# A Conformer layer on one core: the LayerNorm between the last convolution and the second projection, worked in token halves over all channels, with more of the last convolution's taps on the matrix engine

## The chip, the cores and the metric

The kernel runs on one core of a Trainium2 chip. A core has five engines that run side by side, each with its own queue of instructions in a fixed order: TensorE (matrix products, PE in the profile, its weight loads PEld), VectorE (DVE), ScalarE (ACT), GpSimd (POOL) and SyncE (SP), which here only issues transfers. TensorE writes its results into PSUM, eight banks of 512 float32 columns; all else lies in SBUF. The metric is the time of one execution on the device, in microseconds; less is better.

## The reference

One layer for 512 tokens of 2048 channels, all in float32: an RMS norm, a convolution module, a residual, then a squared-ReLU network of inner width 8192, a residual and a last RMS norm. The part that matters here:

```python
def conformer_conv(h, w_pw1, b_pw1, w_dw, b_dw, ln_g, ln_b, w_pw2, b_pw2):
    u = h @ w_pw1 + b_pw1
    a, gate = jnp.split(u, 2, axis=-1)
    u = a * jax.nn.sigmoid(gate)
    u = lax.conv_general_dilated(
        u, w_dw[:, None, :], window_strides=(1,),
        padding=[(CONV_WIDTH // 2, CONV_WIDTH // 2)],
        dimension_numbers=("NWC", "WIO", "NWC"),
        feature_group_count=D_MODEL) + b_dw
    u = jax.nn.silu(layer_norm(u, ln_g, ln_b))
    return u @ w_pw2 + b_pw2
```

The convolution has 31 taps for each channel. The layer norm takes its mean and variance over the 2048 channels of a token, so nothing of it can start for a token before the last channels have gone through the convolution.

## The kernel before, in words

Channels lie on the 128 partitions in 16 tiles (k or j = 0 to 15), tokens along the free dimension. A float32 product is made of three reduced-precision ones: each operand is split into a high part (a cast on ScalarE, `split_hi` for weights) and a low part (a subtraction on VectorE or GpSimd, `split_lo`); `mm3` issues high times high, high times low, low times high. The weights come in pieces of 512 KB (`wr`); a piece of the second projection holds two k tiles for 512 output channels.

**First projection and convolution.** For each channel tile j, `pw1` projects into two PSUM banks (pa and pg), `glu` makes the gated signal u, and `conv` sums 31 taps: some as a ScalarE product and a GpSimd add (`on_pool`), the rest as VectorE multiply-adds in two PSUM banks (`on_vector`), joined at the end. From the third tile on, the VectorE chain starts from `kb`, a bank of its own tag that holds a shift near the mean. `sums` adds value and square to running sums S and Q on GpSimd.

**The last tile (j = 15) is worked in token halves**, half 0 being tokens 0 to 255 and half 1 the rest. `pw1` runs for 272 tokens and then for the other 240 (as 256 columns). Of half 0's taps 7 are on GpSimd, 7 on TensorE (`conv_pe`: matmuls with a diagonal weight, `dgw`; in float32 each is two instructions) and 17 on VectorE; of half 1's 9, 8 and 14. In TensorE's order the taps of half 0 stand behind the whole projection, those of half 1 in three lots among the statistics.

**The layer norm.** Per half: `ln_sums` and `ln_last` sum S, Q, the last two values and squares over the partitions (matmuls of one column, 16 and 8 instructions, into the bank `cols`, which takes over the bank of `kb`); `ln_m2`, `ln_var`, `ln_guard` and `ln_power` make the inverse deviation on ScalarE, VectorE and GpSimd; `ln_mean` and `ln_scale` spread mean and deviation over the partitions by matmuls with diagonal matrices, and ScalarE copies the mean to SBUF. A unit (k, half) is then `ln_a` (GpSimd adds the negative mean), `ln_b` (VectorE multiplies by the deviation, ScalarE does Silu and the cast) and `ln_c` (VectorE subtracts for the low part). Before the change k = 0 to 7 are worked in halves and k = 8 to 15 at full width by `ln(k)`.

**The second projection** has four groups of 512 output channels with four banks each. In the first group the first four pieces (k = 0 to 7) run in halves: half 0 of all four, then half 1 of all four, then the other four pieces at full width. Hooks at given places (`LN_AT`) put the statistics of half 1 among half 0's matmuls: sums at the third piece, mean at the start of the fourth, deviation one block later. Everything behind is dense on TensorE.

**What sets the order.** TensorE's order is the order of the program text throughout. Inside a `manual_schedule(engines=ordered)` block the orders of VectorE, ScalarE and GpSimd are also those of the text; between such blocks, and for everything outside them, a planner merges by its own estimate of times. An engine never passes over a waiting instruction. Tiles of one tag share a ring of buffers: a new one waits until the old user of its buffer is done; the banks `mm` (4), `x` (3) and `y` (1) are such rings.

Of the kernel before, what the change touches and what calls it, by code (L numbers as in the profile page):

```python
# [34 lines left out]
LAST_POOL, LAST_PE = (7, 9), (7, 8)  # L35
# [5 lines left out]
PE_AT = (2, 4)  # L41
SPLIT_AT = (1, 4)
NEXT_AT = 7
TAIL = (20, 7, 4, 2, 3)
LN_AT = ((0, 2, 2), (0, 3, 0), (0, 3, 1))
# [6 lines left out]
def conformer_layer(ctx: ExitStack, tc: tile.TileContext, xT, vecs, wdw, w1, w2, wupb, wdn, outT):  # L52
# [337 lines left out]
    def conv_parts(j, npool, t0=0, n=T, npe=0):  # L390
# [61 lines left out]
    def conv_pe(acce, t0, n, i0, i1, npe):  # L452

        u = ubuf[(NK - 1) % 3]
        for i in range(i0, i1):
# [5 lines left out]
                start=i == 0,  # L461
# [4 lines left out]
    def shift():  # L466
# [3 lines left out]
        nc.tensor.matmul(box["kb"], lhsT=nmean, rhs=vg[0][:, 0, :], start=True, stop=True)  # L470

# [62 lines left out]
    banks_b = pw1(last, HT, HT)  # L534
# [8 lines left out]
    def ln_sums(h):  # L543
        t0 = HT * h
        colsum(cols, 4 * h, [S, box[last - 1][0]], t0, 2, h == 0, False, 1)
        colsum(cols, 4 * h + 2, [Q, box[last - 1][1]], t0, 2, False, False)

    def ln_last(h):
        t0 = HT * h
        colsum(cols, 4 * h, [vlast], t0, 2, False, True, 1)  # L550
        colsum(cols, 4 * h + 2, [sqlast], t0, 2, False, True)
# [4 lines left out]
    def ln_diag_mean(h):  # L556
        st[h]["dm"] = diag(cols[:, 4 * h : 4 * h + 2], f"mu{h}", ph1)

    def ln_mean(h):

        b = rstd[:, 0:HT]
        spread(st[h]["dm"], b, h == 1)
        nc.scalar.copy(out=mus[:, halves[h]], in_=b)

    def ln_m2(h):
        st[h]["m2"] = ph1.tile([P, 2], F32, name=f"m2{h}", bufs=1)
        nc.scalar.activation(out=st[h]["m2"], in_=cols[:, 4 * h : 4 * h + 2], func=AF.Square)

    def ln_var(h):
        st[h]["var"] = ph1.tile([P, 2], F32, name=f"var{h}", bufs=1)  # L570
        nc.vector.tensor_sub(out=st[h]["var"], in0=cols[:, 4 * h + 2 : 4 * h + 4], in1=st[h]["m2"])
# [23 lines left out]
    def ln_b(k, h):  # L595
        t = ph1.tile([P, T], F32, tag=("vt", "ta")[k % 2], name=f"lu{k}_{h}", bufs=2 - k % 2)[:, 0:HT]
# [11 lines left out]
    def ln(k):  # L608
        t = ph1.tile([P, T], F32, tag="pc", name=f"lt{k}")
        nc.gpsimd.tensor_add(out=t, in0=vg[k // 4][:, k % 4], in1=mus)  # L610
        t2 = ph1.tile([P, T], F32, tag="vt", name=f"lu{k}")
        for h in range(2):
            nc.vector.tensor_mul(out=t2[:, halves[h]], in0=t[:, halves[h]], in1=scale_of[h])
        s = ph1.tile([P, T], F32, tag="pm", name=f"ls{k}", bufs=3)
        nc.scalar.activation(out=s, in_=t2, func=AF.Silu, scale=col(C_LNG, k), bias=col(C_LNB, k))
        nc.scalar.copy(out=sh[k], in_=s)
        nc.vector.tensor_sub(out=sl[k], in0=s, in1=sh[k].bitcast(F32))

    with tc.manual_schedule(engines=ordered):

        acc0, rstd = bank("mm", "acce0"), bank("x", "acce1")
        npool, npe = LAST_POOL[0], LAST_PE[0]
        on_pool, on_vector, join, vt, pc = conv_parts(last, npool, 0, HT, npe)
        npool1, npe1 = LAST_POOL[1], LAST_PE[1]
# [8 lines left out]
        for c in range(npool):  # L633
            on_pool(c)
            if c in SPLIT_AT:
                split_hi(n_p1 + 1 + SPLIT_AT.index(c))
        for c in range(npool, TAIL[0]):
            on_vector(c)
        conv_pe(acc0, 0, HT, 0, npe, npe)
        glu(last, *(b[:, EDGE - HT : HT] for b in banks_b), EDGE)  # L640
        some(1)
        cols = bank("y", "cols")
        scale_of = cols[:, HT:T], rstd[:, HT:T]
        ln_sums(0)
        conv_pe(rstd, HT, HT, 0, PE_AT[0], npe1)
        for c in range(TAIL[0], CW - npe - 2):
            on_vector(c)
        v = vlast[:, halves[0]]
        nc.vector.tensor_add(out=v, in0=pc[-1], in1=acc0[:, halves[0]])
        for c in range(CW - npe - 2, CW - npe):  # L650
            on_vector(c)
        join()
        nc.vector.tensor_add(out=v, in0=v, in1=vt)

        for c in range(5):
            on_pool1(c)
            if c == 2:
                split_hi(n_p1 + 3)
        ln_square(0)
        for c in range(5, TAIL[1]):  # L660
            on_pool1(c)
        some(TAIL[2])
        ln_last(0)
        conv_pe(rstd, HT, HT, PE_AT[0], PE_AT[1], npe1)
        ln_m2(0)
        ln_diag_mean(0)
        ln_var(0)
        ln_guard(0)
        ln_power(0)
        some(3)  # L670
        ln_mean(0)

        nc.scalar.activation(out=tiny, in_=ones[:, 0:1], func=AF.Silu)
        ln_diag_scale(0)
        ln_scale(0)
        conv_pe(rstd, HT, HT, PE_AT[1], npe1, npe1)
        ln_a(0, 0)
        ln_a(1, 0)
        for c in range(TAIL[1], npool1):
            on_pool1(c)  # L680
        some(TAIL[3])
        for k in range(0, 8, 2):
            if k < 6:
# [375 lines left out]
```

## Time and profile before

| | |
|---|---|
| median of 3 runs (lowest to highest) | 1942.48 us (1941.43 to 1949.83) |
| the profiled execution's own time, its span | 1946.38 us, 1944.6 us |
| granted TensorE clock, mean | 0.992 |
| TensorE busy | 1913.9 us, 98% |
| VectorE, ScalarE, GpSimd busy | 1389.9 (71%), 741.1 (38%), 356.7 us (18%) |
| HBM read, written | 193.27 MB, 4.19 MB |

The span runs from the first to the last instruction; 1.8 us lie around it. The busy share is a mean over the whole run and says little of the short stretch between the first and the second projection, which comes at about 350 to 436 us. The granted clock has two levels, 1.00 (2.4 GHz) and half of it; a mean between them says for what share of a stretch the clock was low.

### The profile page before, as it was taken

Reading aid. Unit: us, or ns where it says so; the run is one execution under the profiler, and the core shown is the slowest. Engines: PE = TensorE matmul, PEld = TensorE weight load, DVE = VectorE, ACT = ScalarE, POOL = GpSimd, SP = SyncE. Lnnn points to the kernel's source line nnn. Section 1 sums busy time; section 2 is a strip of 40 time slices with the busy share of each in tenths; the row PEclk is TensorE's granted clock in tenths of the full one; section 3 lists DMA queues with packets and bytes.
Section 4 is the critical chain, followed back from the end, with each engine's and each line's share of the span. In section 5 each row is a group of like instructions: output and inputs, shape, how many; then the busy total and the mean of one; then the engine's idle time right before and its main releaser. Section 6 shows DMA issues by size and latency. Waiting matters only on the chain.

```text
span 1944.6 us, 27603 instructions
## 1 busy us (share of the span) xinstructions
PE 1913.9 (98%) x11192; PEld 1702.6 (88%) x11192; DVE 1389.9 (71%) x1911; ACT 741.1 (38%) x907; POOL 356.7 (18%) x243
## 2 busy tenths in 40 slices
PE   9999999899999999999999999999999999999997
PEld 7888888888879898998989899898989989899987
DVE  6999999875467675766767576676757667576844
ACT  6544444554344232423324233332423324242443
POOL 1789998741120000000000000000000000000000
PEclk9999999999999999999999999999999999999999
DMA  7332333143322333333233232323323233332332
GB/s 245 98 98 87 98 98 110 43 141 96 98 78 79 117 101 91 113 87 110 86 108 109 88 119 79 118 87 103 115 87 109 87 119 93 92 116 89 109 98 99
DMA packets 134558, 199.23 MB, mean 102 GB/s; under 512 B 7200, under 2 KB 72992, under 8 KB 134432
## 3 DMA queue, kind: packets, MB, share of 16 engines
q1 hardware_dynamic: 134288, 197.41, 33.1%
q8 instruction: 87, 1.43, 0.3%
q14 instruction: 39, 0.32, 0.1%
q10 hardware_dynamic: 144, 0.07, 0.0%
HBM read 193.27 MB, written 4.19 MB: 102 GB/s over the span
## 4 chain that ended last, share of the span: by engine, by line
issue 70%; PE 25%; DVE 4%; ACT 1%; POOL 1%; DMA 0%; SPq 0%; POOLq 0%; DVEq 0%; ACTq 0%
PE g L201 3%; PE g L202 3%; PE g L200 3%; PE pa L202 2%; PE pa L201 2%; PE pa L200 2%; PE pg L202 2%; PE pg L201 2%; PE pg L200 2%; DVE acc L426 2%; PE pa L363 1%; PE pg L363 1%; DVE slot L604 0%; POOL Q L841 0%; DMA wr<-w 0%
## 5 line engine op out<-in xcount | busy, mean ns | idle before, releaser
L162 ACT CAST wh<-wr 128x1024 fp32r<-128x1024 f32 x215 | 226.0, 1051 | 451.0 <-PE g L201 315.3
L200 PE MATMUL g<-z,wh 128*128 128x512 f32 (+1 forms) x1016 | 390.6, 384 | 0.0
L201 PE MATMUL g<-z,wh 128*128 128x512 f32 (+1 forms) x1016 | 390.3, 384 | 0.0
L202 PE MATMUL g<-z,wl 128*128 128x512 f32 (+1 forms) x1016 | 390.1, 384 | 0.0
L167 DVE TENSOR_TENSOR wl<-wr,wh 128x1024 fp32r<-128x1024 f32 x157 | 197.1, 1256 | 214.4 <-ACT wh L162 214.2
L202 PE MATMUL u<-slot,wl 128*128 128x256 f32 x1120 | 320.1, 286 | 3.6 <-DVE wl L186 2.6
L200 PE MATMUL u<-slot,wh 128*128 128x256 f32 x1120 | 318.1, 284 | 0.0
L201 PE MATMUL u<-slot,wh 128*128 128x256 f32 x1120 | 317.9, 284 | 0.0
L186 DVE TENSOR_TENSOR wl<-ws,wh 128x1024 fp32r<-128x1024 f32 x128 | 156.9, 1225 | 188.0 <-ACT wh L185 187.0
L248 POOL TENSOR_TENSOR rr_fin<-ms_fin,mhalf 128x2 f32<-128x2 f32 x2 | 1.4, 697 | 1341.5 <-DVE ms_fin L246 1341.5
L185 ACT CAST wh<-ws 128x1024 fp32r<-128x1024 f32 x128 | 134.4, 1050 | 289.9 <-DVE ws L183 135.1
L426 DVE SCALAR_TENSOR_TENSOR acc<-u,wd,acc 128x512 f32<-128x512 f32 (+1 forms) x362 | 239.0, 730 | 3.2 <-ACT acc L422 2.5
L202 PEld LDWEIGHTS g<-z,wl 128*128 128x128 f32 x1016 | 190.9, 188 | 37.8
L200 PEld LDWEIGHTS g<-z,wh 128*128 128x128 f32 x1016 | 191.0, 188 | 37.5
L201 PEld LDWEIGHTS g<-z,wh 128*128 128x128 f32 x1016 | 191.0, 188 | 37.1
L202 PEld LDWEIGHTS u<-slot,wl 128*128 128x128 f32 x1120 | 216.1, 193 | 7.4 <-DVE wl L186 6.6
L200 PEld LDWEIGHTS u<-slot,wh 128*128 128x128 f32 x1120 | 216.2, 193 | 0.0
L201 PEld LDWEIGHTS u<-slot,wh 128*128 128x128 f32 x1120 | 216.1, 193 | 0.0
L202 PE MATMUL u<-T,wl 128*128 128x256 f32 x672 | 190.6, 284 | 1.6 <-DVE wl L186 1.5
L200 PE MATMUL u<-T,wh 128*128 128x256 f32 x672 | 190.7, 284 | 1.0 <-ACT wh L185 1.0
L201 PE MATMUL u<-T,wh 128*128 128x256 f32 x672 | 190.1, 283 | 0.0
L178 ACT CAST wh<-wr 128x768 fp32r<-128x768 f32 x128 | 106.9, 835 | 214.5 <-PE g L201 123.0
(199 smaller groups left out, 3448.8 us busy)
## 6 DMA issues: line engine op xcount, KB each, us to landing
wr<-wupb SPq DMA_DIRECT2D x128, 512.0 KB, 3.6
wr<-wdn SPq DMA_DIRECT2D x128, 512.0 KB, 3.7
wr<-w SPq DMA_DIRECT2D x128, 256.0 KB, 3.2
wr<-w SPq DMA_DIRECT2D x32, 512.0 KB, 3.6
h<-xT SPq DMA_DIRECT2D x4, 1024.0 KB, 11.3
outT<-h SPq DMA_DIRECT2D x14, 256.0 KB, 2.8
x<-xT SPq DMA_DIRECT2D x6, 512.0 KB, 8.1
x<-xT SPq DMA_DIRECT2D x4, 256.0 KB, 4.9
```

The source lines that it names most:

```text
L162: nc.scalar.copy(out=prepped[i][0], in_=r)
L167: eng.tensor_tensor(out=lo, in0=r, in1=hi.bitcast(F32), op=ALU.subtract)
L178: nc.scalar.copy(out=hr, in_=r[:, :, 1:4])
L185: nc.scalar.copy(out=hs, in_=s)
L186: nc.vector.tensor_tensor(out=ls, in0=s, in1=hs.bitcast(F32), op=ALU.subtract)
L200: nc.tensor.matmul(out, lhsT=wh, rhs=xh, start=start, stop=False, **kw)
L201: nc.tensor.matmul(out, lhsT=wh, rhs=xl, start=False, stop=False, **kw)
L202: nc.tensor.matmul(out, lhsT=wl, rhs=xh, start=False, stop=stop, **kw)
L248: nc.gpsimd.tensor_tensor(out=r, in0=ms, in1=mhalf[:, 0:n], op=ALU.pow)
L363: nc.tensor.matmul(banks[j][s], lhsT=w[:, s, k % 2, c], rhs=x, start=k == 0 and x is ah[k] and w is wh, stop=stop)
L426: nc.vector.scalar_tensor_tensor(out=acc if c < end - 1 else vt, in0=u[:, c : c + n], scalar=wd[:, j, c : c + 1], in1=src, op0=ALU.mult, o ...
```

## The change

- For the last tile TensorE takes 10 taps of half 0 and 14 of half 1; VectorE is left with 14 and 8. The taps of half 0 are now emitted from within the second projection half of the last tile, ahead of its k = 8 (`first_taps`, hooked at `LAST_AT`), and the bank for them is taken from the ring ahead of the two banks of that half.
- The second half of the shift is copied to SBUF (`kbs`), so that `kb`'s bank has no reader left when the column sums of half 0 want it. Each half has its own bank for its four columns of sums (`stat`): `cols` for half 0, the bank of half 1's TensorE taps for half 1. The sums of half 1 are made together, at the hook.
- All 16 channel tiles go through the layer norm in halves, as one list of 32 units (`units`): first k = 0 to 15 of half 0, then of half 1. `ln_step` issues the adds up to three units ahead, the multiply, Silu and cast of the next unit and the subtraction of the one before. In the main block the conv taps of half 1 stand between the steps; `ln(k)` goes.
- The first group runs five pieces in halves. The sums of half 1 come ahead of the fifth piece of half 0, its mean and deviation ahead of half 1's first piece.
- The low parts of weight pieces 3 and 4 of this projection are made on VectorE instead of GpSimd; that of piece 1 comes earlier.

```diff
-LAST_POOL, LAST_PE = (7, 9), (7, 8)
+LAST_POOL, LAST_PE = (7, 9), (10, 14)
...
-LN_AT = ((0, 2, 2), (0, 3, 0), (0, 3, 1))
+LAST_AT = 8
+PE_FIRST = 6
+SPLIT = 5
+LN_AT = ((0, 4, 0), (HT, 0, 0))
...
-                src = box["kb"][:, t0 : t0 + n]
+                src = box["kbs"] if t0 else box["kb"][:, 0:n]
...
+        box["kbs"] = ph1.tile([P, HT], F32, name="kbs", bufs=1)
+        nc.scalar.copy(out=box["kbs"], in_=box["kb"][:, HT:T])
...
+    units = [(k, h) for h in range(2) for k in range(NK)]
+    done = {"a": 0, "b": 0}
...
+    def ln_step(ahead=NK):
+        n = done["b"]
+        while done["a"] < min(n + 3, ahead):
+            ln_a(*units[done["a"]])
+            done["a"] += 1
+        ln_b(*units[n])
+        done["b"] += 1
+        if n:
+            ln_c(*units[n - 1])
...
+    acc0 = bank("mm", "acce0")
+    on_pool, on_vector, join, vt, pc = conv_parts(last, npool, 0, HT, npe)
+
+    def first_taps():
+        with tc.manual_schedule(engines=ordered):
+            for c in range(npool):
+                on_pool(c)
+                if c in SPLIT_AT:
+                    split_hi(n_p1 + 1 + SPLIT_AT.index(c))
+            for c in range(npool, CW - npe):
+                on_vector(c)
+            conv_pe(acc0, 0, HT, 0, npe, npe, True)
+
+    banks_b = pw1(last, HT, HT, hooks={LAST_AT: first_taps})
+    cols, rstd = bank("y", "cols"), bank("x", "acce1")
+    stat, scale_of = (cols, rstd), (cols[:, HT:T], rstd[:, HT:T])
     with tc.manual_schedule(engines=ordered):
+        join()
         v = vlast[:, halves[0]]
         nc.vector.tensor_add(out=v, in0=pc[-1], in1=acc0[:, halves[0]])
         nc.vector.tensor_add(out=v, in0=v, in1=vt)
         ln_square(0)
+        ln_sums(0)
         ln_last(0)
+        glu(last, *(b[:, EDGE - HT : HT] for b in banks_b), EDGE)
         ln_m2(0)
         ln_diag_mean(0)
         ln_var(0)
         ln_guard(0)
         ln_power(0)
         ln_mean(0)
         nc.scalar.activation(out=tiny, in_=ones[:, 0:1], func=AF.Silu)
+        split_lo(n_p1 + 1, nc.vector)
         ln_diag_scale(0)
...
+        conv_pe(rstd, HT, HT, 0, PE_FIRST, npe1, False)
         ln_scale(0)
+        conv_pe(rstd, HT, HT, PE_FIRST, npe1, npe1, False)
+        some(2)
+        for c in range(2):
             on_pool1(c)
+        for n in range(9):
+            ln_step()
+            if n < 7:
+                on_pool1(2 + n)
+                some(1)
+            if n == 3:
+                split_hi(n_p1 + 3)
+                split_lo(n_p1 + 2, nc.vector)
+            if n == 6:
                 v = vlast[:, halves[1]]
                 nc.vector.tensor_add(out=v, in0=pc1[-1], in1=rstd[:, halves[1]])
                 some(99)
                 join1()
                 nc.vector.tensor_add(out=v, in0=v, in1=vt1)
                 ln_square(1)
+                split_lo(n_p1 + 3, nc.vector)
+                split_hi(n_p1 + 4)
+        split_lo(n_p1 + 4, nc.vector)

     def second_sums():
+        ln_sums(1)
         ln_last(1)
         with tc.manual_schedule(engines=ordered):
             ln_m2(1)
+            ln_step()
             ln_diag_mean(1)
             ln_var(1)
             ln_guard(1)
             ln_power(1)
+            ln_step()
+            ln_step()
             ln_diag_scale(1)
...
     def second_scale():
         with tc.manual_schedule(engines=ordered):
+            ln_mean(1)
+            ln_scale(1)
+            while done["b"] < 2 * NK:
+                ln_step(2 * NK)
+            ln_c(*units[-1])
         p1.close()
...
-        banks = group(NK, sh, sl, hooks, split=4 if g == 0 else 0)
+        banks = group(NK, sh, sl, hooks, split=SPLIT if g == 0 else 0)
```

## Rows read from the trace of the kernel before

**Rows 1.** Waits of TensorE: who waited for whom; total us, times, longest us
```profile
PE g L201 <- DVE slot L604: 3.7, 5, 2.3
PE g L201 <- DVE slot L617: 3.0, 1, 3.0
```

**Rows 2.** Stretches: length, busy us (instructions) by engine, granted clock, DMA share, GB/s
```profile
core 0: us, PE busy (x) PEld busy (x) DVE busy (x) ACT busy (x) POOL busy (x), PEclk, DMA share, GB/s
347.22:358.70 11.48, 11.48 (x98) 11.48 (x97) 11.31 (x22) 7.40 (x12) 9.53 (x9) 1.00 0.01 2
358.70:375.83 17.13, 15.50 (x76) 12.99 (x75) 14.69 (x39) 10.69 (x23) 12.31 (x18) 0.80 0.00 0
375.83:409.50 33.67, 29.77 (x206) 28.14 (x206) 24.51 (x46) 18.44 (x37) 20.36 (x20) 0.90 0.17 48
...
412.92:436.20 23.28, 23.28 (x96) 19.11 (x96) 16.40 (x24) 10.01 (x14) 5.16 (x3) 0.93 0.81 281
436.20:458.00 21.80, 21.80 (x98) 18.06 (x97) 15.58 (x16) 11.13 (x14) 6.12 (x4) 1.00 0.33 106
```

**Rows 3.** Timeline of TensorE: start, length, engine, line, operation, count, idle before
```profile
347.57 0.28 PE L200 MATMUL pg<-slot,wh 128*128 128x256 f32 x1
...
358.73 3.18 PE L457 MATMUL acce<-u,dgw 128*128 128x256 f32 x14
363.54 0.58 PE L234 MATMUL cols<-invd,S 128*128 128x1 f32 x4 [1.63 <-DVE acc L426]
...
365.31 1.27 PE L457 MATMUL acce<-u,dgw 128*128 128x256 f32 x4
...
386.26 0.38 PE L201 MATMUL g<-slot,wh 128*128 128x256 f32 x1 [2.28 <-DVE slot L604]
```

**Rows 4.** Timeline of VectorE
```profile
347.59 0.43 DVE L380 TENSOR_TENSOR ta<-pa,rmix 128x272 f32<-128x272 f32 x1
...
365.31 0.42 DVE L436 TENSOR_TENSOR vt<-vt,acc 128x256 f32<-128x256 f32 x1
...
380.92 1.21 DVE L167 TENSOR_TENSOR wl<-wr,wh 128x1024 fp32r<-128x1024 f32 x1
...
383.57 2.96 DVE L604 TENSOR_TENSOR slot<-ls,slot 128x256 fp32r<-128x256 f32 x2 [0.78 <-ACT slot L600]
...
408.00 3.17 DVE L167 TENSOR_TENSOR wl<-wr,wh 128x1024 fp32r<-128x1024 f32 x1 [0.79 <-ACT wh L162]
```

**Rows 5.** Timeline of GpSimd
```profile
371.43 1.41 POOL L592 TENSOR_TENSOR lt<-v,mus 128x256 f32<-128x256 f32 x2 [1.42 <-ACT mus L563]
...
383.58 2.35 POOL L167 TENSOR_TENSOR wl<-wr,wh 128x1024 fp32r<-128x1024 f32 x1
```

**Rows 6.** Timeline of ScalarE
```profile
368.15 0.17 ACT L567 ACTIVATE m<-cols 128x2 f32<-128x2 f32 x1 [0.71 <-PE cols L234]
...
371.31 1.28 ACT L673 ACT_TABLE_LOAD   x1
...
390.22 0.17 ACT L567 ACTIVATE m<-cols 128x2 f32<-128x2 f32 x1 [1.77 <-PE cols L234]
...
395.42 0.60 ACT L599 ACTIVATE ls<-lu,vec 128x256 f32<-128x256 f32 x1 [1.31 <-DVE lu L597]
...
402.31 0.60 ACT L599 ACTIVATE ls<-lu,vec 128x256 f32<-128x256 f32 x1 [0.34 <-DVE lu L597]
```

**Rows 7.** Groups, 360 to 440 us: busy us, mean ns of one, idle before
```profile
L592 POOL TENSOR_TENSOR lt<-v,mus 128x256 f32<-128x256 f32 x16 | 12.4, 802 | 8.2 <-DVE lu L597 4.7 <-ACT mus L563 3.5
L411 POOL TENSOR_TENSOR pc<-pc,pm 128x256 f32<-128x256 f32 x10 | 7.5, 748 | 1.3 <-DVE lu L597 0.4 <-ACT pm L409 0.2
...
L604 DVE TENSOR_TENSOR slot<-ls,slot 128x256 fp32r<-128x256 f32 x16 | 12.1, 763 | 3.4 <-ACT slot L600 3.2
...
L600 ACT CAST slot<-ls 128x256 fp32r<-128x256 f32 x16 | 6.5, 406 | 0.4
L409 ACT ACTIVATE pm<-u,wd 128x256 f32<-128x256 f32 x9 | 4.1, 496 | 0.3 <-POOL pc L411 0.3
```

**Rows 8.** DMA issues of the page: count, KB each, median us to landing
```profile
h<-xT SPq DMA_DIRECT2D x4, 1024.0 KB, 11.3
```

More of the change, by code (lines that the diff above doesn't have):

```diff
@@ L450, in conv, with conv_pe @@
         nc.gpsimd.tensor_add(out=vg[j // 4][:, j % 4], in0=vt, in1=pc[-1])
-    def conv_pe(acce, t0, n, i0, i1, npe):
+    def conv_pe(acce, t0, n, i0, i1, npe, start):
         u = ubuf[(NK - 1) % 3]
@@ L460, in conv_pe @@
                 rhs=u[:, t0 + c : t0 + c + n],
-                start=i == 0,
+                start=start and i == 0,
                 stop=i == npe - 1,
@@ L543, in ln_sums @@
     def ln_sums(h):
-        t0 = HT * h
-        colsum(cols, 4 * h, [S, box[last - 1][0]], t0, 2, h == 0, False, 1)
-        colsum(cols, 4 * h + 2, [Q, box[last - 1][1]], t0, 2, False, False)
+        t0, cols = HT * h, stat[h]
+        colsum(cols, 0, [S, box[last - 1][0]], t0, 2, True, False, 1)
+        colsum(cols, 2, [Q, box[last - 1][1]], t0, 2, False, False)
     def ln_last(h):
-        t0 = HT * h
-        colsum(cols, 4 * h, [vlast], t0, 2, False, True, 1)
-        colsum(cols, 4 * h + 2, [sqlast], t0, 2, False, True)
+        t0, cols = HT * h, stat[h]
+        colsum(cols, 0, [vlast], t0, 2, False, True, 1)
+        colsum(cols, 2, [sqlast], t0, 2, False, True)
     def ln_square(h):
@@ L556, in ln_diag_mean @@
     def ln_diag_mean(h):
-        st[h]["dm"] = diag(cols[:, 4 * h : 4 * h + 2], f"mu{h}", ph1)
+        st[h]["dm"] = diag(stat[h][:, 0:2], f"mu{h}", ph1)
     def ln_mean(h):
         b = rstd[:, 0:HT]
-        spread(st[h]["dm"], b, h == 1)
+        spread(st[h]["dm"], b)
         nc.scalar.copy(out=mus[:, halves[h]], in_=b)
@@ L566, in ln_m2 @@
         st[h]["m2"] = ph1.tile([P, 2], F32, name=f"m2{h}", bufs=1)
-        nc.scalar.activation(out=st[h]["m2"], in_=cols[:, 4 * h : 4 * h + 2], func=AF.Square)
+        nc.scalar.activation(out=st[h]["m2"], in_=stat[h][:, 0:2], func=AF.Square)
     def ln_var(h):
         st[h]["var"] = ph1.tile([P, 2], F32, name=f"var{h}", bufs=1)
-        nc.vector.tensor_sub(out=st[h]["var"], in0=cols[:, 4 * h + 2 : 4 * h + 4], in1=st[h]["m2"])
+        nc.vector.tensor_sub(out=st[h]["var"], in0=stat[h][:, 2:4], in1=st[h]["m2"])
     def ln_guard(h):
@@ L606, in ln_c @@
         )
[L608 to L617, printed above, removed]
@@ L619, in conformer_layer @@
-    with tc.manual_schedule(engines=ordered):
[L621 to L624, printed above, removed]
+    def ln_step(ahead=NK):
[7 more added lines that the diff above has]
+            ln_c(*units[n - 1])
@@ new lines, in conformer_layer @@
+    npool, npe = LAST_POOL[0], LAST_PE[0]
+    npool1, npe1 = LAST_POOL[1], LAST_PE[1]
+    acc0 = bank("mm", "acce0")
[9 more added lines that the diff above has]
+            conv_pe(acc0, 0, HT, 0, npe, npe, True)
@@ new lines, in conformer_layer @@
+    banks_b = pw1(last, HT, HT, hooks={LAST_AT: first_taps})
+    cols, rstd = bank("y", "cols"), bank("x", "acce1")
+    stat, scale_of = (cols, rstd), (cols[:, HT:T], rstd[:, HT:T])
+    with tc.manual_schedule(engines=ordered):
+        join()
+        v = vlast[:, halves[0]]
+        nc.vector.tensor_add(out=v, in0=pc[-1], in1=acc0[:, halves[0]])
+        nc.vector.tensor_add(out=v, in0=v, in1=vt)
+        ln_square(0)
+        ln_sums(0)
+        ln_last(0)
+        glu(last, *(b[:, EDGE - HT : HT] for b in banks_b), EDGE)
+        ln_m2(0)
+        ln_diag_mean(0)
+        ln_var(0)
+        ln_guard(0)
+        ln_power(0)
+        ln_mean(0)
+        nc.scalar.activation(out=tiny, in_=ones[:, 0:1], func=AF.Silu)
+        split_lo(n_p1 + 1, nc.vector)
+        ln_diag_scale(0)
@@ L631, in some @@
                     on_vector1(taps.pop(0))
[L633 to L655, printed above, removed]
-            on_pool1(c)
-            if c == 2:
-                split_hi(n_p1 + 3)
[L659 to L683, printed above, removed]
-                ln_a(k + 2, 0)
-                ln_a(k + 3, 0)
-            ln_b(k, 0)
-            ln_b(k + 1, 0)
-            if k == 0:
-                ln_sums(1)
-            if k == 2:
+        conv_pe(rstd, HT, HT, 0, PE_FIRST, npe1, False)
+        ln_scale(0)
+        conv_pe(rstd, HT, HT, PE_FIRST, npe1, npe1, False)
+        some(2)
+        for c in range(2):
+            on_pool1(c)
+        for n in range(9):
[4 more added lines that the diff above has]
+            if n == 3:
+                split_hi(n_p1 + 3)
+                split_lo(n_p1 + 2, nc.vector)
+            if n == 6:
                 v = vlast[:, halves[1]]
```

36 lines of the change are left out of this document (4 added, 32 removed).

## The prediction, made before the changed kernel was run

> **What bounds the kernel now.** I read the waits of TensorE first, then stretches of the run with the granted clock, then the timelines of single engines around the stretch that the change touches. TensorE hardly waits: behind the first pairs its longest waits are for the low parts of the LayerNorm output, 3.7 us in five pieces and 3.0 us in one [rows 1]. So only what stands on TensorE's own queue counts, and of that only the stretch from the second half of the last pair's projection (starts at 347.22 us) to the end of the first output group (436.20 us). In the next group 96 matmuls of 512 columns take 21.80 us at clock 1.00, 0.227 us each [rows 2]; from there on the kernel after should run like the one before. The stretch lasts 89.0 us. The projection half is dense (96 matmuls of 256 columns in 11.48 us, 0.12 each). Behind it TensorE stands 1.63 us until 363.54 for the shift bank that the column sums reuse, 2.28 us until 386.26 and 3.0 us until 412.92 [rows 1, 3], and its clock is low three times: (1 - clock) x length gives 3.4 us lost in 358.70 to 375.83, 3.4 in 375.83 to 409.50 and 1.6 in 412.92 to 436.20 [rows 2]. The low level is 1.2 of 2.4 GHz, and each low stretch follows one of the three waits. Waits and low clock come to some 15.3 us; that is all there is to win, and 0.5% of the run, about what a measurement of this kernel can tell from no change, is 9.7 us.
>
> The two later waits have causes on VectorE. At 383.57 two subtractions take 2.96 us together while GpSimd runs the split of a weight piece, 2.35 us [rows 4, 5]; the split at 408.00 takes 3.17 us where the one at 380.92 took 1.21 [rows 4].
>
> **The change, part by part.** Times below continue the clock of the profiled execution.
>
> *Projection half with taps inside.* Ten taps of token half 0 go between the two parts of the projection. A tap is two instructions: 14 in 3.18 us, 0.227 each [rows 3]. 20 x 0.227 = 4.5 us. The accumulator bank now comes between the two halves' banks, so the gate bank of the second half is the one from which VectorE reads pa at 347.59 to 348.02, while TensorE wants it at 347.57 [rows 3, 4]: 0.5 us (0.4 to 1.4, if VectorE reads the other first). The half ends at 358.7 + 0.5 + 4.5 = 363.8. VectorE has three taps fewer on half 0; its sum is ready a few tenths before that, so what it saves is hidden behind TensorE.
>
> *Statistics of half 0.* The column sums no longer wait for the shift bank (1.63 us gone): late next is the projection itself. 16 column sums take 1.77 us [rows 3], 24 take 2.7: 366.5. From the square of the mean at 368.15 to the table load at 371.31 it took 3.2 us, at low clock [rows 6]; I allow 1.7 (clock full) to 3.2: 368.2 to 369.7. Then the table load (1.28), a tiny activation (0.2) and the first two products of half 1 (0.5 each) on ScalarE and one add on GpSimd (0.75) stand ahead of the first LayerNorm add [rows 6, 7]: it starts at 371.4 to 372.9; before, it started at 371.43, straight behind the mean [rows 5]. The three microseconds that the statistics gain are spent here.
>
> *Half 0 as a pipeline.* From there to the last GpSimd add of half 1, GpSimd has nine LayerNorm adds (0.80) and seven conv adds (0.75) in its queue [rows 7]: 12.5 us, 383.9 to 385.4. VectorE adds the TensorE taps, joins and adds (3 x 0.43 [rows 4]), splits a weight piece (1.2), and only then comes the step of k = 7: multiply 0.4, Silu 0.6, cast 0.41, subtract 0.76 [rows 4, 6, 7]. All that is written ahead of it on VectorE's queue, so the low part of k = 7 lands at 388.6 to 390.1. TensorE needs it for the last 20 of the 24 matmuls of the fourth weight piece (k = 6 and 7; 2.4 us): 391.0 to 392.5. Its own 14 taps of half 1 (28 x 0.227 = 6.4 us) end at 375 to 378 and don't decide. The two splits taken off GpSimd remove the 2.28 us wait; the new late thing in the same place is the order on VectorE.
>
> *Statistics of half 1.* 16 + 8 column sums, 2.7 us: T0 = 393.7 to 395.2. The square of the mean waits on ScalarE for them, as it did at 390.22 (1.77 us [rows 6]); behind it on the same queue now stand the Silu and cast of k = 9 to 11, half 0. TensorE's next piece needs k = 9: 0.2 + 0.6 + 0.41 + 0.76 = 2.0 us, then 20 matmuls, 2.4: T0 + 4.4. Two spreads of two instructions: T0 + 5.3.
>
> *Start of half 1.* Its mean is copied by ScalarE only now (about T0 + 5.5), and behind that copy stand k = 12 to 15 of half 0, which TensorE wants much later, ahead of k = 0 of half 1. Silus of successive channels started 1.15 us apart (395.42 to 402.31, six steps [rows 6]); back to back they would be 0.95. Four: 4.6 us (3.8). Then 1.8 us for Silu, cast and subtract, one unit more, and 20 matmuls: TensorE ends the first piece of half 1 at T0 + 15.4 (14.3). Four pieces at 24 x 0.12 and three of full width at 24 x 0.227 add 27.9: T0 + 43.3 (42.2). Before, this place cost nothing: the mean was spread inside the piece ahead and k = 0 came first.
>
> *Sum.* 435.9 to 438.5 at full clock, middle 437.2. The wait at the start of half 1, some 5 us, is longer than any that has been followed by low clock here; such a stretch cost 1.6 to 3.4 us [rows 2]; I take 2.5: 439.7, against 436.2. That is 3.5 us more: span 1948.1 us, and 1949.9 with the 1.8 us around it. The profiled execution lies 3.9 us above the median of the runs, so I forecast 1946.0 for that median.
>
> *Costed at nothing.* Six more diagonal weights of 128x128 on ScalarE (each under a cast of 128x256, 0.41 [rows 7]: 0 to 2.5 us): TensorE has the first pairs' projections before it. The copy of half of the shift (about 0.4 us, as a cast [rows 7]) hides beside a dense pair. The split of piece 1, now ahead of the scale's diagonal on VectorE, delays it some 0.3 us beside 2.7 us of taps; it releases its buffer earlier, and the load that SP then issues falls where the DMA share is 0.00 [rows 2]. One more piece in halves is 24 x (2 x 0.12 - 0.227) = 0.3 us, inside the sum. The last LayerNorm add, which releases memory for the residual loads, comes near T0 + 27 (15 units behind the first of half 1), 422; the loads land in 11.3 us [rows 8], ahead of the group's end near 440, where they are first read. The halves of k = 8 to 15 cost ScalarE more (2 x 1.0 against 1.4 us), under TensorE's 2.9 us for two units. No third wait of 3.00 us is due: by then LayerNorm is some units ahead.
>
> *A rule weighed against the trace.* Subtractions on VectorE have a mean of 0.76 us [rows 7] where the split at 380.92 shows how the engine runs without company, and two took 2.96 beside the 2.35 us instruction on GpSimd [rows 4, 5]: one waits for the other. The Trainium skill says so in SBUF — State Buffer, section "SBUF: two separate sides": a VectorE instruction with two SBUF inputs and a GpSimd instruction that reads SBUF exclude each other for their whole length. The trace agrees; where it bites in the new order is the third rival.
>
> **The rivals.**
> 1. *The waits go and nothing takes their place.* If ScalarE has k = 12 to 15 out of the way and both halves flow: minus 2.28, minus 3.00, minus 3.4 and 1.6 of clock, plus 9 taps (4.1), the bank (0.5) and the piece in halves (0.3): 5.4 us less, 1937.1. For it: the two causes on VectorE are plain. Against: the written order puts the copy of the mean ahead of four units that aren't needed yet.
> 2. *Slower: low clock twice.* If the wait for k = 6 and 7 (from about 385 to 389) also drops the clock, the rest of that piece and the column sums run at half, and the statistics gate everything behind: 3.4 us there, 3.4 after the start of half 1, on the late end of the sum: 438.5 + 6.8 = 445.3, 9.1 us more, 1951.6. It decides as soon as a wait there is as long as the 2.28 us one was; what follows still counts in full, because half 1 can't start before those sums. A planner that also puts a split into the first units of half 1 takes it over 1952.2.
> 3. *GpSimd and VectorE exclude each other in the pipeline.* If in the seven steps each subtraction (0.41 alone) and one split (1.2) hold GpSimd up, its queue is 4.1 us longer; with T0 that much later, and the rest as forecast: 7.6 us more, 1950.1. Against: GpSimd's adds have a mean of 0.80, so so far it is VectorE that waits [rows 7]. By the section of the Trainium skill named above it depends on which instruction starts first.
> 4. *Nothing moves*, the losses and gains equal: 1942.5.
>
> **How the numbers follow.** Forecast (between 1943.5 and 1949) 0.42; rival 4 (1940 to 1943.5) 0.17; rival 1 0.15, of which 0.04 is more than 9.7 us, for which all three low stretches would have to go; rival 3 0.12; rival 2 and worse 0.14, of which 0.10 is beyond 9.7 us. So faster by over 0.5% 0.04, slower by over 0.5% 0.10, within 0.86. The range leaves out most of rival 1's far end and the worst of rival 2: 1938.5 to 1952.5. The forecast's own range, from full clock and early T0 to late T0 and both clock losses, is 1942.2 to 1951.6.
>
> **What would show it.** Right: no wait of some 2.3 us behind a GpSimd split; a projection half of about 16.5 us; a wait in the fourth piece behind the subtractions of k = 6 and 7; a wait of about 5 us at the first piece of half 1, ended by a subtraction, with four Silus between the mean's copy and that of k = 0; low clock behind it; no wait in the three full pieces; the group ending near 440. Wrong: if half 1 starts within 2 us of its spreads, or if the statistics of half 1 are summed well before 393.

## The result and the profile after

The changed kernel takes 1956.55 us (median of 5, 1955.84 to 1961.38), the kernel before in the same sitting 1945.75 (median of 5, 1941.43 to 1949.83): ratio 1.0061, 95% interval 1.0041 to 1.0081. The forecast was 1946.0 and the range ended at 1952.5, so the time lies outside. Slower, by 0.6%, where "within 0.5%" had most of the chance.

The profiled execution of the changed kernel is that median, 1956.55 (span 1954.8 against 1944.6 before). The stretch of the prediction, from the first matmul of the projection's second half to the group's end, is now 96.0 us where it was 89.0. Its windows (length, busy time by engine, granted clock, DMA) answer to [rows 2]:

```profile
core 0: us, PE busy (x) PEld busy (x) DVE busy (x) ACT busy (x) POOL busy (x), PEclk, DMA share, GB/s
349.28:365.10 15.82, 15.82 (x119) 15.28 (x118) 15.58 (x32) 8.54 (x14) 12.73 (x13) 1.00 0.01 2
365.10:377.00 11.90, 10.72 (x55) 8.96 (x54) 6.47 (x17) 5.83 (x13) 4.88 (x6) 0.86 0.15 44
377.00:398.90 21.90, 17.91 (x125) 16.60 (x124) 14.27 (x26) 11.74 (x24) 12.75 (x16) 0.92 0.14 49
398.90:411.00 12.10, 7.11 (x28) 5.61 (x28) 7.63 (x18) 7.42 (x17) 6.65 (x9) 0.66 0.01 2
411.00:445.30 34.30, 33.41 (x192) 29.80 (x193) 21.30 (x40) 20.82 (x39) 10.48 (x13) 0.92 0.54 184
```

The projection half is dense, 15.8 us. In the fourth window TensorE works 7.1 of 12.1 us, at clock 0.66: a place where it hardly waited before. TensorE's waits in the stretch, in place of [rows 1]:

```profile
PE g L201 <- ACT slot L604: 5.4, 3, 4.5
PE g L202 <- DVE slot L608: 4.0, 4, 2.3
```

The two long ones are the two that the prediction named. TensorE's timeline shows them in the fourth weight piece and at the first piece of half 1 (number in brackets: idle before, and who ended it):

```profile
390.60 0.39 PE L202 MATMUL g<-slot,wh 128*128 128x256 f32 x1 [2.26 <-DVE slot L608]
...
392.17 0.38 PE L202 MATMUL g<-slot,wh 128*128 128x256 f32 x1 [0.44 <-DVE slot L608]
396.16 0.50 PE L235 MATMUL acce<-invd,S 128*128 128x1 f32 x4
...
400.08 0.58 PE L201 MATMUL g<-slot,wh 128*128 128x256 f32 x1 [0.72 <-ACT slot L604]
404.98 1.05 PE L224 MATMUL acce<-dg_mu,ones 128*128 128x256 f32 x2
406.50 0.70 PE L224 MATMUL acce<-dg_lnr,ones 128*128 128x256 f32 x2 [0.46 <-ACT mus L564]
411.65 0.58 PE L201 MATMUL g<-slot,wh 128*128 128x256 f32 x1 [4.45 <-ACT slot L604]
```

Between 392.17 and 396.16 TensorE waits for nothing; the rest of one piece takes it 3.99 us. VectorE's timeline shows why k = 6 and 7 are late: the join of half 1's value stands ahead of their low parts and waits 2.02 us for GpSimd's ninth tap.

```profile
387.53 0.42 DVE L686 TENSOR_TENSOR v<-pc,acce 128x256 f32<-128x256 f32 x1 [2.02 <-POOL pc L412]
...
390.13 0.42 DVE L608 TENSOR_TENSOR slot<-ls,slot 128x256 fp32r<-128x256 f32 x1
...
391.32 0.79 DVE L608 TENSOR_TENSOR slot<-ls,slot 128x256 fp32r<-128x256 f32 x1
```

ScalarE's timeline, beside [rows 6], has the square of half 1's mean, the copy of the mean, and behind it the Silus of k = 12 to 15 of half 0 ahead of k = 0 of half 1 (the last row):

```profile
398.94 0.17 ACT L568 ACTIVATE m<-acce 128x2 f32<-128x2 f32 x1 [6.71 <-PE acce L235]
...
406.07 0.37 ACT L564 COPY mus<-acce 128x256 f32<-128x256 f32 x1 [3.90 <-PE acce L224]
406.34 0.60 ACT L603 ACTIVATE ls<-lu,vec 128x256 f32<-128x256 f32 x1
...
410.56 0.60 ACT L603 ACTIVATE ls<-lu,vec 128x256 f32<-128x256 f32 x1
```

The span grew by 10.2 us: 2.1 ahead of the stretch, 7.05 in it and 1.1 behind it. A second profile of the same kernel, e0 below, has 0.2, 7.1 and 3.1. So the 7 us repeat; the rest is looked into below.

To see where in the stretch they lie, split it at T0, the start of the square of half 1's mean (390.22 before, 398.94 after). Before and after, columns as above:

```profile
347.22:390.22 43.00, 37.95 (x241) 34.53 (x240) 36.92 (x76) 23.87 (x46) 27.95 (x31) 0.88 0.13 38
390.22:436.20 45.98, 42.51 (x233) 37.29 (x233) 33.41 (x53) 26.00 (x43) 22.22 (x18) 0.93 0.42 145
```
```profile
349.28:398.94 49.66, 44.49 (x295) 40.88 (x294) 36.31 (x73) 26.12 (x51) 30.35 (x34) 0.93 0.10 33
398.94:445.31 46.37, 40.49 (x221) 35.38 (x221) 28.95 (x57) 28.24 (x55) 17.14 (x21) 0.85 0.40 137
```

T0 does not stand at the same place of TensorE's work in the two. The change puts 36 more matmuls of half 0 ahead of it (4.3 us at 0.12 each) and nine taps (4.1 us): 8.4 us more work there, and T0 comes 6.7 us later, with the same waits (length minus busy: 5.2 us, 5.1 before) and less low clock ((1 - clock) x length: 3.5 us, 5.2 before). Behind T0 it leaves 4.0 us less work (12 matmuls of 256 columns more, 24 of 512 fewer), and that part still takes 0.4 us longer: waits 5.9 us against 3.5, low clock 7.0 against 3.2, some of it within the waits. So TensorE got 4.4 us more work, and the waits that should have paid for it grew from 8.5 to 11.05 us, at the start of half 1.

### The profile page after: what moved, and what is told of

Read it like the earlier page. It is cut to its first block, busy times and chain, and to the rows that moved or that the text cites. A ratio compares the mean times of both kernels' runs of the same rounds, so it can differ in the third digit from the quotient of the medians.

```text
span 1954.8 us, 27726 instructions
## 1 busy us (share of the span) xinstructions
PE 1921.1 (98%) x11234; PEld 1709.3 (87%) x11234; DVE 1386.5 (71%) x1912; ACT 747.4 (38%) x930; POOL 351.4 (18%) x249
## 4 chain that ended last, share of the span: by engine, by line
issue 69%; PE 28%; DVE 1%; POOL 1%; ACT 0%; DMA 0%; POOLq 0%; SPq 0%; DVEq 0%
PE g L202 3%; PE g L201 3%; PE g L203 3%; PE pa L201 3%; PE pg L201 3%; PE pa L203 3%; PE pg L203 3%; PE pa L202 3%; PE pg L202 3%; PE pa L364 1%; PE pg L364 1%; PE acce L458 0%; POOL pc L412 0%; DVE h L969 0%; DMA wr<-w 0%
```

## The experiments

Three theories. **A**: ScalarE's order, mean copy and four units of half 0 ahead of half 1, keeps TensorE waiting at the start of half 1. **B**: TensorE's own added work (nine taps, a piece in halves) lengthens the stretch. **C**: low clock behind the waits lengthens what comes next. For each profile the table has three lengths: from the first matmul of the projection's second half (b) to T0; from T0 to G, the first matmul of the second output group on TensorE, which ends the stretch (the 97th matmul of 512 columns in the second projection for before, e2, g3 and g4, the 73rd in the others); and from G to the end of the span. The recorded expectations count to r, the first row of the residual on VectorE. In ten profiles r lies 1.84 us ahead of G; in the four with e1's order of units (e1, e5, g1, g2) it lies from 0.3 us ahead of G to 0.2 behind it (VectorE's row in e1 and e5 names the residual's load as what it waits for), so that there the way to r hides 1.5 to 2.1 us of what TensorE gained. The ratio is to the kernel before on the same chip; "order" is explained at g3. Each profile is one execution of its kernel, and single executions of one kernel lie up to 10 us apart (e7: 1948.69 to 1958.47).

```
                      median   ratio [95%]               b-T0   T0-G   b-G    G-end    order
before                1945.75  1                        43.00  45.98  88.98  1508.40  cast first
after                 1956.55  1.0061 [1.0041, 1.0081]  49.66  46.37  96.03  1509.49  square first
e0_after              1957.60  1.0069 [1.0054, 1.0083]  49.64  46.43  96.07  1511.51  square first
e1_unit_order         1952.54  1.0036 [1.0023, 1.0048]  48.64  44.03  92.67  1506.81  cast first
e2_before_vector_..   1943.46  0.9989 [0.9980, 0.9997]  39.68  46.73  86.41  1507.48  cast first
e3_busy               1953.09  1.0044 [1.0031, 1.0058]  48.16  44.37  92.53  1512.23  square first
e4_taps_back          1961.40  1.0076 [1.0064, 1.0088]  54.21  47.19 101.40  1511.43  square first
e5_order_and_busy     1949.44  1.0010 [1.0002, 1.0019]  49.77  42.39  92.16  1508.71  cast first
e6_vector_order       1957.49  1.0056 [1.0044, 1.0068]  54.16  47.13 101.29  1511.49  square first
e7_spread_earlier     1952.73  1.0033 [1.0020, 1.0047]  49.90  43.45  93.35  1508.68  cast first
g1_order_and_spread   1948.21  1.0005 [0.9996, 1.0014]  52.16  39.82  91.98  1508.15  cast first
g2_order_spread_busy  1949.58  1.0016 [1.0007, 1.0025]  49.49  40.38  89.87  1511.46  square first
g3_before_shift_copy  1947.29  1.0006 [0.9997, 1.0014]  38.85  47.45  86.30  1511.90  square first
g4_before_shift_busy  1944.18  0.9990 [0.9981, 0.9999]  39.80  46.83  86.63  1509.57  cast first
```

**e0_after** is the changed kernel again.

> The changed kernel again, unaltered, beside the experiments on the same chip. Its stretch from the last projection half to the end of the first output group was 96.0 us against 89.0 before, and 2.1 us more lay in its first 11 us, where the first weights landed 0.5 us later and the TensorE clock was low until 10.2 us. If the start is chance, it differs from run to run in either kernel and this profile need not show it; the stretch should again be 95 to 97 us. If the start belongs to the change, it shows again.

1.0069: it repeats. b-T0 and T0-G agree with the first profile within 0.1 us. All 14 profiles have b between 346.6 and 349.3, kernels of either kind at both ends (after 349.28, e0 347.42, before 347.22, e2 348.71): the 2.1 us ahead of the stretch are not the change's.

**e1_unit_order** takes theory A's units out of the way.

```diff
-    units = [(k, h) for h in range(2) for k in range(NK)]
+    units = [(k, 0) for k in range(12)] + [(k, 1) for k in range(12)]
+    units += [(k, h) for k in range(12, NK) for h in range(2)]
...
-        tag = ("tg", "ta", "lt")[(16 * h + k) % 3]
+        tag = ("tg", "ta", "lt")[units.index((k, h)) % 3]
...
-    def ln_step(ahead=NK):
+    def ln_step(ahead=12):
```

> Only the order of the 32 LayerNorm units differs from the changed kernel: k = 0 to 11 of half 0, k = 0 to 11 of half 1, then k = 12 to 15 with both halves of each. Theory A (ScalarE works k = 12 to 15 of half 0 ahead of k = 0 of half 1, right behind the copy of the mean): the 4.5 us wait at the first piece of half 1 shrinks to about 1 us, the low clock behind it shortens, the stretch is 4 to 6 us shorter than the changed kernel's 96.0. Theory B (the loss is TensorE's own added work, 9 taps at 0.45 us and one more piece in halves, 4.4 us): the stretch stays within 1.5 us of 96.0.

TensorE's wait at the start of half 1 falls from 4.45 to 1.70 us, as A says, and T0-G by 2.4 us; the stretch is 3.4 us shorter than e0's, short of the 4 to 6 that A would have given, and this profile is the fastest of e1's eight runs (1948.59).

```profile
405.56 0.55 PE L201 MATMUL g<-slot,wh 128*128 128x256 f32 x1 [1.70 <-ACT slot L605]
```

From the end of that wait to G it takes 34.4 us, in e0 33.7, in e3 32.5: in the 10 us behind it the clock is 0.66, in e0 0.75, in e3 1.00. VectorE's row for r shows the load that it waits for:

```profile
439.70 2.73 DVE L808 SCALAR_TENSOR_TENSOR h<-g,vec,h 128x512 f32<-128x512 f32 x4 [2.87 <-DMA h<-xT]
```

**e2_before_vector_splits** is the kernel before with one part of the change, the splits of two weight pieces on VectorE.

```diff
-        split_lo(n_p1 + 3, nc.gpsimd)
+        split_lo(n_p1 + 3, nc.vector)
...
-                    split_lo(n_p1 + 4, nc.gpsimd)
+                    split_lo(n_p1 + 4, nc.vector)
```

> The kernel before with one part of the change: the low parts of weight pieces 3 and 4 of the second projection are made on VectorE instead of GpSimd. If the wait of 2.28 us before was VectorE held up by GpSimd's 2.35 us split, as the prediction has it, that wait and the low clock behind it go: 4 to 6 us less than before. Rival: the two splits, 1.2 us each on VectorE's own queue, take back what they give: within 1.5 us of before.

T0 comes 3.3 us earlier, the stretch is 2.6 us shorter, and the kernel is 0.03 to 0.2% faster than the one before: less than the 4 to 6 us expected. The wait of 2.28 us is gone; in its place TensorE waits 2.67 us for the spread of half 1's scale. Low parts like the two that took 2.96 us together [rows 4] now take 0.43 each, on VectorE's timeline:

```profile
384.92 0.43 DVE L604 TENSOR_TENSOR slot<-ls,slot 128x256 fp32r<-128x256 f32 x1 [0.78 <-ACT slot L600]
385.86 0.43 DVE L604 TENSOR_TENSOR slot<-ls,slot 128x256 fp32r<-128x256 f32 x1 [0.52 <-ACT slot L600]
```

So the prediction read the cause of that wait rightly. By the Trainium skill, SBUF — State Buffer, section "SBUF: two separate sides", a GpSimd instruction that reads SBUF and a VectorE instruction with two SBUF inputs exclude each other; these rows agree.

**e3_busy** tests C: matmuls on a tile of zeros fill TensorE's two waits.

```diff
+FILL = (20, 36)
...
+        fill(FILL[1])
         p1.close()
...
+            hooks[0, 3, 0] = lambda: fill(FILL[0])
```

> The changed kernel with matmuls of a zero operand put on TensorE where it waits: 20 (about 2.4 us) ahead of the fourth piece of half 0 and 36 (about 4.3 us) ahead of the first piece of half 1. They add zeros to a bank of the group, and nothing waits for them. Theory C (a good part of the loss is the low clock that follows the waits, not the waits): the clock stays at 1.00 through the statistics of half 1 and the first pieces of half 1, and the stretch is 3 to 6 us shorter than 96.0. Theory A alone: the waits are filled but end when they ended before, within 1 us of 96.0.

3.5 us of the 7.1 are gone, 1.5 ahead of T0 and 2.1 behind it, with more work on TensorE. From the fourth piece's last wait to the column sums it now takes 2.50 us (389.53 to 392.03) instead of 3.99. Windows of 5 us, columns as above:

```profile
390.00:395.00 5.00, 5.00 (x46) 5.00 (x44) 0.95 (x2) 0.20 (x2) 0.00 (x0) 1.00 0.10 34
395.00:400.00 5.00, 4.20 (x22) 3.79 (x22) 4.41 (x11) 2.78 (x6) 3.87 (x5) 0.72 0.00 0
400.00:405.00 5.00, 4.54 (x33) 4.04 (x32) 2.68 (x7) 3.48 (x8) 1.81 (x3) 0.94 0.01 2
405.00:410.00 5.00, 3.87 (x26) 3.06 (x26) 3.86 (x9) 4.32 (x10) 3.62 (x6) 1.00 0.00 0
410.00:415.00 5.00, 5.00 (x45) 5.00 (x44) 3.93 (x9) 4.33 (x10) 3.62 (x6) 1.00 0.01 3
```

In e0 the same five windows have 0.66, 0.77, 0.55, 0.79 and 0.53. ScalarE's order is that of e0, so it is the clock that gave this.

**e4_taps_back** tests B.

```diff
-LAST_POOL, LAST_PE = (7, 9), (10, 14)
+LAST_POOL, LAST_PE = (7, 9), (7, 8)
```

> The changed kernel with the last pair's taps shared out as before (7 and 8 on TensorE instead of 10 and 14), all else as changed. Theory B (the nine added taps, about 4.5 us of TensorE in the projection half and the half-1 taps, are what lengthens the stretch): 3 to 4.5 us less than the changed kernel. Theory A and C (the units ahead of half 1 on ScalarE, and the low clock behind the waits): VectorE carries 3 and 6 more taps of 0.41 us in their place, the value of half 1 comes later, and the time is the same or up to 3 us more than the changed kernel's.

Longer by 5.3 us in the stretch, not shorter: VectorE, with nine more taps, lets the fourth piece wait 4.35 us, and T0 is 4.6 us later. So B fails as the thing to undo: the nine taps are 4.1 us of the added work, and in this order they pay for themselves.

```profile
389.74 0.39 PE L202 MATMUL g<-slot,wh 128*128 128x256 f32 x1 [4.35 <-DVE slot L608]
```

**e5_order_and_busy** is e1 and e3 together (20 and 14 matmuls on zeros).

> The changed kernel with both earlier edits: the units k = 12 to 15 of half 0 behind k = 11 of half 1, and matmuls on a tile of zeros (20 ahead of the fourth piece, 14 at the start of half 1) in TensorE's waits; neither changes the result. If the place of the four units and the low clock are two causes, their gains of the stretch (1.85 us and 3.5 us alone) add: 88.5 to 89.5 us from the first matmul of half b to the first row of the residual, against 94.2, and with the instruction order in the FFN stage as before (2.1 us of waits less) a total 6.5 to 8 us under the changed kernel. If the low clock is only what follows the wait that the units make, little is left to add: 90.5 or more, and the total within 2 us of the better of the two alone.

Counted to r, as the expectation has it, the stretch is 92.31 us, which speaks for its second case; but r waits for its load here. On TensorE the gains behind T0 nearly add: T0-G is 4.0 us under e0's, against 2.4 in e1 and 2.1 in e3. b-T0 is 1.6 us over e3's, since this profile has clock 0.66 in 365 to 375 us, where e3's has 0.83, in code that the two share. The medians add too: over the kernel before of its sitting e0 lies 11.9 us, e1 6.8, e3 7.4 and e5 2.0 (in e1 and e5 with the other order in the FFN stage, see g3). So A and C are two causes.

**e6_vector_order** moves the join of half 1's value behind the low part of k = 6.

```diff
-            if n == 6:
+            if n == 7:
...
-                split_lo(n_p1 + 3, nc.vector)
-                split_hi(n_p1 + 4)
+        split_lo(n_p1 + 3, nc.vector)
+        split_hi(n_p1 + 4)
```

> The changed kernel with the block that joins half 1's value put behind unit 7's multiplication and unit 6's low part in VectorE's order (it stood ahead of them and waits 2.0 us for GpSimd's ninth tap), and its two operand splits behind the last unit step. If that wait of VectorE is what holds the fourth piece (2.26 us), the fourth piece waits 0 to 1.2 us, the sums of half 1 and all behind them come 1 to 2 us earlier, and the total is 1 to 3 us less (the clock may come back earlier too). If the fourth piece is held by ScalarE's two steps of units 6 and 7 instead, nothing changes.

No gain in the median (1957.49), and no verdict on the wait: the two splits that I put last made a new one in the same piece, and the clock fell behind it. The profiled execution was the longest of the six (1963.29), so its 101.29 us overstate the stretch.

```profile
392.87 0.58 PE L203 MATMUL g<-slot,wl 128*128 128x256 f32 x1 [3.30 <-DVE wl L168]
```

**e7_spread_earlier** shortens theory A's chain at its head.

```diff
-LN_AT = ((0, 4, 0), (HT, 0, 0))
+LN_AT = ((0, 4, 0), (0, 4, 2))
```

> The changed kernel with the spread of half 1's mean and scale moved from behind the fifth piece to its middle (behind 12 of its 24 matmuls). If the copy of the mean on ScalarE, and the four units behind it, set the start of half 1, the copy comes about 2 us earlier, the wait ahead of half 1's first piece (4.45 us) falls to 2 to 3 us, and the total is 1.5 to 3.5 us less, and 2.1 us less again if the FFN stage keeps the order of before. If the scale's chain (power on GpSimd) is what is late, TensorE waits in the middle of the piece instead and the total is the same.

The mean is copied 4.6 us behind T0 instead of 7.1, the wait falls to 3.18 us, T0-G by 3.0 us. A is a true cost of the place. Mean copy on ScalarE, and the wait on TensorE:

```profile
401.55 0.37 ACT L564 COPY mus<-acce 128x256 f32<-128x256 f32 x1 [1.34 <-PE acce L224]
```
```profile
407.27 0.39 PE L201 MATMUL g<-slot,wh 128*128 128x256 f32 x1 [3.18 <-ACT slot L604]
```

**g1_order_and_spread** is e1 and e7 together; **g2_order_spread_busy** the same with zeros (20 ahead of the fourth piece, 8 at half 1's start).

> The changed kernel with the unit order of e1 (k = 12 to 15 of half 0 behind k = 11 of half 1) and the earlier spread of e7 (middle of the fifth piece). The two act on the same chain (the copy of half 1's mean and what ScalarE does behind it), so if that chain sets the start of half 1 they add only in part: stretch from the first matmul of half b to the first row of the residual 90 to 91 us against 94.2 (92.4 and 91.5 alone). ScalarE's order in the FFN stage is that of the kernel before, so the 2.4 us of weight waits there fall away: 2 to 5 us over the kernel before. If the low clock and not the chain is the cause, the stretch stays at 91.5 or more.

> The same with matmuls on zeros in TensorE's waits (20 ahead of the fourth piece, 8 at the start of half 1); the result is not changed. If the low clock is a cause of its own: stretch 87.5 to 89 us, 2 us or more under the run without the zeros. In the FFN stage ScalarE's order here has the activation of the first unit ahead of a weight cast, as in the changed kernel: from the first row of the residual to the end 2.4 us longer than in the run without the zeros, so that the totals of the two come out within 1 us of one another.

T0-G falls to 39.8 and 40.4, some 6 us under the kernel before, where the work is 4.0 us less. T0 stays 9.2 and 6.5 us later than there; 8.4 us of that are the work put ahead of it. g1's stretch missed the 90 to 91 us expected: its clock ahead of T0 is 0.87, e0's 0.93. In the median g1 can't be told from the kernel before (0.9996 to 1.0014): the order of the units and the place of the spread, with the order in the FFN stage that came with them, take back all but some 1.6 us of the loss (1948.21 against 1946.65). g2's stretch is 2.1 us shorter than g1's (2 or more expected, though the level of 87.5 to 89 was missed), and its way from G to the end 3.3 us longer: 1.4 us more in total.

**g3_before_shift_copy** and **g4_before_shift_busy** are e2 with the change's copy of the shift in SBUF, g4 with 18 matmuls on zeros ahead of the spread of half 1's scale.

```diff
-                src = box["kb"][:, t0 : t0 + n]
+                src = (box["kbs"] if t0 else box["kb"][:, 0:n])
...
+        box["kbs"] = ph1.tile([P, HT], F32, name="kbs", bufs=1)
+        nc.scalar.copy(out=box["kbs"], in_=box["kb"][:, HT:T])
```

> The kernel before with the two operand splits on VectorE (as e2) and the changed kernel's copy of the shift in SBUF. If the copy takes away TensorE's wait for the shift's bank (1.63 us) and nothing is late behind it: stretch 83 to 84 us against 84.6 of e2; if VectorE's chain of half 0's value is what counts, 84.6 again. ScalarE's order in the FFN stage is here that of the changed kernel: if that order costs weight waits by itself, the rest from the first row of the residual to the end is 2 to 3 us longer than e2's although nothing else of the change is in this kernel, and the total 0.5 to 2.5 us over e2's.

> The same with 18 matmuls on zeros ahead of the spread of half 1's scale (the wait there is 2.67 us, and TensorE runs at low clock for 5 us behind it); the result is not changed. ScalarE's order in the FFN stage is that of the kernel before. If low clock behind a wait is what it seems: stretch 1 to 2 us under the run without the zeros, and the total 3 to 4 us under it, 3 to 5 us under the kernel before. If the clock does not matter: the same stretch, and 2 to 3 us less for the order alone.

Their stretches are equal to e2's within 0.3 us. The wait for the shift's bank (1.63 us) went, and one of 1.65 for half 0's value took its place; the zeros took the wait for the scale from 2.66 to 0.58 us, and the clock from 390 to 395 us from 0.66 to 1.00, but the wait in half 1's fourth piece stood at 2.80 in both: VectorE's chain gave the gain back. Yet in the median g4 is 3.1 us faster than g3 (its profile, 1946.69, is the slowest of its eleven runs). This is the last column of the table. In the first feed-forward unit, 170 us behind the stretch and in code that no kernel here changes, the planner sets ScalarE's square of the unit's result either ahead of a weight cast or behind it; VectorE's order differs at the same place, and from 20 us behind r on nothing else differs in the 14 kernels on ScalarE, VectorE and GpSimd. In g3, ScalarE and then TensorE:

```profile
600.80 1.06 ACT L902 ACTIVATE c<-c 128x1024 f32<-128x1024 f32 x1 [6.16 <-DVE ws L183]
601.77 1.03 ACT L185 CAST wh<-ws 128x1024 fp32r<-128x1024 f32 x1
```
```profile
602.85 0.38 PE L200 MATMUL u<-T,wh 128*128 128x256 f32 x1 [1.65 <-ACT wh L185]
604.11 0.38 PE L202 MATMUL u<-T,wl 128*128 128x256 f32 x1 [0.76 <-DVE wl L186]
```

In g4 the same two places:

```profile
601.21 1.05 ACT L186 CAST wh<-ws 128x1024 fp32r<-128x1024 f32 x1 [4.58 <-PE u L203]
602.16 0.83 ACT L179 CAST wh<-wr 128x768 fp32r<-128x768 f32 x1
602.89 1.05 ACT L917 ACTIVATE c<-c 128x1024 f32<-128x1024 f32 x1
```
```profile
603.57 0.39 PE L203 MATMUL u<-T,wl 128*128 128x256 f32 x1 [0.15 <-DVE wl L187]
```

Windows of 120 us, each from 130 us behind its kernel's r, g3's and then g4's:

```profile
561.17:681.17 120.00, 110.40 (x705) 100.50 (x704) 83.79 (x115) 45.04 (x52) 11.85 (x5) 0.97 0.29 88
```
```profile
563.49:683.49 120.00, 112.95 (x718) 102.66 (x717) 86.52 (x120) 45.07 (x52) 11.85 (x5) 0.97 0.29 88
```

TensorE stands 2.55 us longer in g3, at the same clock. In such a window TensorE is busy 112.5 to 114.9 us in the seven profiles with the cast first (113.08 in the kernel before) and 110.4 to 112.1 in the seven with the square first (110.69 in e0). In the table, G-end is 1508.3 us on average with the cast first (1506.8 to 1509.6) and 1511.4 with the square first (1509.5 to 1512.2). No run changes this order alone; that it costs some 3 us rests on these two groups and on g3 against g4.

## Why the prediction was wrong

**What held.** A projection half of about 16.5 us, 15.8 measured, without the bank wait; no wait behind a GpSimd split; a wait in the fourth piece behind VectorE's order; a wait of some 5 us at the first piece of half 1 with four Silus between the copy of the mean and k = 0 (4.45 us, ended by the cast of k = 0 and not by its subtraction); low clock behind it; no wait in the three full pieces; and the direction, slower than the kernel before. The first LayerNorm add comes at 373.25, 371.2 on the prediction's clock (2.06 us less), against 371.4 to 372.9. Rival 3, put at 4.1 us on GpSimd's queue, came to about 1: from the first add to the ninth tap the queue takes 14.25 us (373.25 to 387.50) where 12.5 were forecast, 1.18 of it a wait for ScalarE's product. The nine LayerNorm adds take 7.5 us instead of 7.2, the seven conv adds 6.0 instead of 5.25 [rows 7]; one add takes 1.71 beside VectorE's split of 1.37 at 380.12.

```profile
373.25 2.10 POOL L596 TENSOR_TENSOR lt<-v,mus 128x256 f32<-128x256 f32 x3
376.52 0.73 POOL L412 TENSOR_TENSOR pc<-pc,pm 128x256 f32<-128x256 f32 x1 [1.18 <-ACT pm L410]
...
380.36 1.71 POOL L596 TENSOR_TENSOR lt<-v,mus 128x256 f32<-128x256 f32 x1
```

**What failed in the stretch: T0.** The prediction put it at 393.7 to 395.2 and it came at 398.94 - 2.06 = 396.9, 2.4 us behind the middle. 0.7 of that is the low part of k = 7, at 392.11 - 2.06 = 390.05, the late end of its bounds. 1.6 is the last 20 matmuls of the fourth piece, counted at 2.4 us and measured at 3.99, nearly all at half clock: it is low behind the wait of 2.26 us, as the prediction's rival 2 has it ("as long as the 2.28 us one was"), and e3 gives back 1.5. That rival had 0.14 where the trace of before already showed a wait of the same length followed by clock 0.66 (385 to 395 us).

**What failed in the stretch: the clock term behind T0.** The sum has T0 + 42.75 at its middle and 2.5 us for one stretch of low clock, T0 + 45.25; measured is T0 + 46.4, 1.1 us more. The fifth piece of half 0 ran at low clock too, so that the mean was copied at T0 + 7.1 and not 5.5; the four Silus took 4.2 us to k = 0, within the 3.8 to 4.6 of the sum, and 0.5 us came back behind them. The prediction allowed low clock once, 2.5 us in all. It came at three places: in the rest of the fourth piece, in the fifth, and at the start of half 1 (in e0, 0.66 in 390 to 395 us, 0.55 in 400 to 405, 0.53 in 410 to 415). The measured end of the stretch, 445.3 - 2.06 = 443.2, lies between the forecast's 439.7 and rival 2's 445.3.

The main argument of the forecast, four units ahead of half 1, held: behind T0 the change leaves TensorE 4.0 us less work and takes 0.4 us longer, and e7 and g1 take 3.0 and 6.6 us out of that part by the order alone.

**What failed outside: "from there on the kernel after should run like the one before."** It does not; the planner's other order goes with some 2 us more of waits there (2.55 in g3 against g4) and some 3 us of time. It was put at nothing and had no rival. Why the planner's estimate tips is open: both orders occur on either side, and matmuls on zeros (g2, g4) or a copy (g3) go with a change of it.

**The base.** The forecast leaned on a median of 1942.48; five runs have 1945.75, and 33 in the last sitting 1946.65. The profiled execution, 1946.38, was the better guide: 3.3 us of the miss. The account of the miss of 10.55 us: base 3.3, stretch 7.05 - 3.5 = 3.55, order about 3, and 0.7 that I can't assign, within the spread of a kernel's runs.

## What to carry to other kernels

A wait ahead of something that gates the next stage is to be priced twice, as itself and as half speed through that gate; the same low clock ahead of another wait cost nothing (g3 against g4). Where a planner merges part of the program, a change can reorder code far behind it: compare the instruction order of the whole program, not of the edited stage. Split a stretch where the same work lies on both sides, and time it on the engine that bounds it: T0 moved against TensorE's work, and r against TensorE's end. And read a change by its parts: of the two that ran alone on the kernel before, the splits moved to VectorE paid (e2, 0.9989), and the copy of the shift added nothing in the stretch (g3).

## What the runs showed of the hardware

The same instructions can have another clock from one execution to the next: the first six taps of half 1 (12 matmuls) take 3.87 us in the changed kernel, 3.93 in e0 and 5.34 in e5 and g1, each time behind one-column matmuls and waits of 0.72 and 0.46 us. The Trainium skill, TensorE: Matmul & The Clock Gate, section "HAM oscillation — how this bites in real kernels", tells of waits after which the next piece starts slow; the traces agree for 2.26 and 4.45 us, and show low clock behind the short ones here too. Matmuls on zeros, at 0.12 us each, held the clock at 1.00 through 390 to 395 us where it had been 0.66.
